# One Trainium2 core, a two-layer hybrid decoder trunk: the first attention unit's scores inside the next product, queries in an even and an odd tile, and a later split of one weight tile

## The chip, the core and the metric

The kernel runs on one core of a Trainium2 chip. A core has five engines with a queue each: TensorE (PE in the profile; its weight loads are PEld), VectorE (DVE), ScalarE (ACT), GpSimd (POOL) and SyncE (SP). Each works through its own queue in order, and semaphores hold an instruction back until what it reads is there. Transfers are issued from the queues of SP, POOL and ACT and run on 16 DMA engines. The metric is the device time of one execution in microseconds (us); lower is better.

## What is computed

A residual stream `x` of 512 tokens by 1024 features goes through two layers in float32. Each layer is a half-weighted SwiGLU, a mixing block and another half-weighted SwiGLU, with an RMSNorm ahead of each and one at the end:

```python
for l in range(2):
    x = x + 0.5 * swiglu(rms_norm(x, ffn1_norm[l]), ffn1_wg[l], ffn1_wu[l], ffn1_wd[l])
    z = rms_norm(x, mix_norm[l]) @ w_in[l]          # 1024 -> q 512 | k 128 | v 128 | conv B, C, h 512 each
    attn = sliding_window_attention(q, k, v, sink)   # 8 query heads of 64, 2 key heads, window 128, blocks of 128 tokens
    conv = B * depthwise_causal_conv3(C * h)
    x = x + concat([attn, conv]) @ w_out[l]
    x = x + 0.5 * swiglu(rms_norm(x, ffn2_norm[l]), ffn2_wg[l], ffn2_wu[l], ffn2_wd[l])   # 1024 -> 2816 -> 1024
return rms_norm(x, final_norm)
```

Attention is computed block by block: a block of 128 queries sees its own 128 keys and the 128 before it, with a linear bias, a learned sink in the softmax's denominator, and probabilities times values.

## The kernel before

**Numbers in two parts.** Every factor of a large product is split into `hi` (a ScalarE cast, line 221, or an activation) and `lo` (what is left, a VectorE subtraction, line 222), and a product is made of three matrix products: hi by hi, hi by lo, lo by hi. So each weight tile of 128x1024 costs ScalarE a cast (`wh<-raw`) and VectorE a subtraction (`wl<-raw,wh`) before TensorE can use it. Weights are loaded into a ring of eight buffers (`raw`, `stock`), which the attention's probability tiles `p` share; `need_split(g)` splits all tiles up to the g-th of a fixed list, and loads four further ahead. `behind(...)` lets instructions be placed only after given others; otherwise a scheduler sets the order on ScalarE and VectorE, and in most places on TensorE.

**The mixing block (`mix`).** `halves` computes keys, values and the first query product in one go. Then come the three other query products (`group(norm.h)`, `j` from 1 to 3, 24 matrix products of 512 columns each; lines 313, 314 and 316), and six pairs of products for the convolution. From each query product, ScalarE copies one half of the partitions and VectorE takes the remainder into the other half, first for the even head (`qe`), then for the odd one (`qo`; lines 1691 and 1692). Attention is cut into eight units, one for each block of queries (four) and key head (two); a unit holds four query heads. `attend(step)` issues the stages of the units that are due in a step: `scores` (eight or so small products into the tiles `sc`, lines 1549 and 1550; then VectorE adds the bias and takes the row maximum, line 1553, and writes `p`; ScalarE takes exponentials, line 1570; VectorE divides, line 1578), then either `turn` (TensorE transposes `pt`, for units 0, 4 and 7) or `apart`, `send` and `join` (two ScalarE copies `pr<-p`, line 1588, a transposing DMA, two ScalarE copies back, line 1609, and the split into `ph` and `pl`, lines 1613 and 1615), and `values` (products `o`, lines 1642 and 1643). The tiles `sc` have two PSUM buffers. The scores of the first unit are issued after query product `j` = 1 and need the heads of `j` = 0 and 1; those of the second unit after `j` = 2.

**From the mixing block into the second SwiGLU.** The output product (`share`) adds into `x` as its parts end. When the last part of a half of the tokens has been added, `Norm.stage` computes the norm of that half: ScalarE's sums of squares, `v` (line 653), ScalarE's reciprocal root `r` (line 654), a Newton step on VectorE (lines 657 and 535 to 537), and the scaled rows `xn` (line 665; two tiles of 128 tokens for each half `o` of the features). TensorE transposes `xn` (`xt`, line 689). `plain_halves` then multiplies by four weight tiles (`held`; products `up`, line 1102), the first half of the tokens first. Between its tiles it pulls the transposes of the second half of the tokens: `o` = 0 after the second tile, `o` = 1 after the third. `hold` splits the third and the fourth of these weight tiles. This transition exists once in each layer, at norms 2 and 5.

**The end (`Finale.down`).** The last two token tiles are closed in an order that is written out by hand for ScalarE and VectorE. The last one is closed in two column pieces; its reciprocal root `r_end` (line 1419) needs `done` (line 1484), which takes in the first piece's sum of squares.

Of the kernel before, what the change touches and what calls it, by code (L numbers as in the profile page):

```python
# [9 lines left out]
F32R = mybir.dt.float32r  # L10
# [6 lines left out]
P = 128  # L17
D = 1024
S = 512
# [56 lines left out]
def trunk_kernel(  # L76
# [254 lines left out]
    def hold(norm, n):  # L331

        first = state["group"]
        if norm.added:
            for ahead, one in ((2, norm.added), (3, norm.first)):
                with behind(one):
                    need_split(first + ahead)
                if norm.later is not None:
                    norm.added = state["sub"]
                    norm.go_on()  # L340
        return [take_split(SPLIT_AHEAD - j)[1:] for j in range(n)]
# [244 lines left out]
    class Norm:  # L586


        def __init__(self, i, gain, mixing, tags):
            self.i, self.row, self.mixing, self.tags = i, gain, mixing, list(tags)  # L590
            self.ss = small(f"ss_{i}", 2 * NT)
            self.seen = [0, 0]
            self.later = self.added = None
            if mixing:
                self.h = None
                return
            self.full = None
# [47 lines left out]
        def stage(self, half):  # L645

            i = self.i
            if half == 0:
                self.rooms()
                self.waiting = []  # L650
            v, r, y = (small(f"{n}_{i}_{half}", 2) for n in "vry")
            at = 2 * half
            nc.vector.tensor_add(v, self.ss[:, at : at + 2], self.ss[:, NT + at : NT + at + 2])
            self.guess = nc.scalar.activation(
                r, v, AF.Abs_reciprocal_sqrt, scale=1.0 / D, bias=eps
            )
            nc.vector.tensor_scalar(v, v, 1.0 / D, EPS, op0=ALU.mult, op1=ALU.add)
            newton(y, r, v)
            self.first = None
            for o in range(2):  # L660
                xns = []
                self.first = self.first or (self.scaled if o else None)
                for t in (at, at + 1):
                    xns.append(g2(f"xn_{i}_{t}_{o}"))
                    self.scaled = nc.vector.scalar_tensor_tensor(
                        xns[-1],
                        xt(t, o),
                        y[:, t - at : t - at + 1],
                        self.gain[o],
                        op0=ALU.mult,  # L670
                        op1=ALU.mult,
                    )
                self.waiting.append((half, o, xns))

        def pull(self):

# [689 lines left out]
    class Finale:  # L1366
# [65 lines left out]
        def down(self, rhs):  # L1432
            for half in range(2):
                gb = g2(f"gain_{half}")
                nc.sync.dma_start(
                    gb, final_norm[half * S : (half + 1) * S].partition_broadcast(P)
                )
                self.gain.append(gb)
            done = small("done", NT)
            self.widen(0, len(rhs) // 2)  # L1440
            for t in range(NT):
                rest = done[:, t : t + 1]
                acc = self.products(rhs, 0, t, 0, S)
                self.close(acc, 0, t, 0, rest)
                nc.vector.tensor_scalar(rest, rest, 1.0 / D, EPS, op0=ALU.mult, op1=ALU.add)
                if t == 0:
                    self.widen(1, len(rhs) // 2)
            def factor(t, ssq):
                return self.root(t, ssq, done[:, t : t + 1])

            def scale(t, by, h):
                y = self.y[t][h]
                if h:
                    nc.vector.scalar_tensor_tensor(
                        y, y, by, self.gain[h], op0=ALU.mult, op1=ALU.mult
                    )
                else:
                    nc.scalar.activation(y, y, AF.Copy, scale=by)
                cols = slice(h * S, (h + 1) * S)
                queue = nc.scalar if h == 0 and t == NT - 1 else nc.sync  # L1460
                queue.dma_start(out[0, t * P : (t + 1) * P, cols], y)

            def piece(t, c0, wide):
                ssq = small(f"ssq_end{t}_{c0}", 1)
                self.close(self.products(rhs, 1, t, c0, wide), 1, t, c0, ssq)
                return ssq

            for t in range(NT - 2):
                by = factor(t, piece(t, 0, S))
                for h in (1, 0):  # L1470
                    scale(t, by, h)


            a, b = NT - 2, NT - 1
            with tc.manual_schedule(engines={act, dve}):
                ssq = piece(a, 0, S)
                early = self.guess(a, ssq, done[:, a : a + 1])
                first = piece(b, 0, H)
                by = self.mend(a, ssq, done[:, a : a + 1], early)
                scale(a, by, 0)  # L1480
                second = piece(b, H, H)
                scale(a, by, 1)
                rest = done[:, b : b + 1]
                nc.vector.scalar_tensor_tensor(
                    rest, first, 1.0 / D, rest, op0=ALU.mult, op1=ALU.add
                )
                by = self.mend(b, second, rest, self.guess(b, second, rest))
                for h in (1, 0):
                    scale(b, by, h)


    def mix(l, norm, after):
# [36 lines left out]
        class Unit:  # L1529
# [8 lines left out]
            def scores(self):  # L1538
# [5 lines left out]
                for i in range(2):  # L1544
                    sc = psum("sc", [P, 2, 2 * P], f"sc_{self.name}_{i}")
                    for j in range(2):
                        h = 2 * i + j
                        qs = q[4 * g + h][:, n * P : (n + 1) * P]
                        nc.tensor.matmul(sc[:, j, lo:], qs, kh[g][:, keys], start=True, stop=False)
                        nc.tensor.matmul(sc[:, j, lo:], qs, kl[g][:, keys], start=False, stop=True)  # L1550
                    for j in range(2):
                        h = 2 * i + j
# [120 lines left out]
        def attend(step, what=(VALUES_AT, TURN_AT, SEND_AT, SCORES_AT)):  # L1673
# [6 lines left out]
                        done = getattr(unit, stages.get(at, "join"))() or done  # L1680
            return done

        for j in range(NH // 2):
            acc = group(norm.h) if j else qacc
            if j == 3:
                vv = take_values()
            if j % 2 == 0:
                room = both(f"q_{l}_{j}", shape=(P, 2, 2, S))
            qe, qo = room[j % 2][:, 0, :], room[j % 2][:, 1, :]
            for z, a, b in ((qe, slice(0, HD), slice(HD, P)), (qo, slice(HD, P), slice(0, HD))):  # L1690
                nc.scalar.activation(z[a, :], acc[a, :], AF.Copy, scale=1.0 / 8.0)
                nc.vector.scalar_tensor_tensor(
                    z[b, :], acc[a, :], 1.0 / 8.0, f32(z[a, :]), op0=ALU.mult, op1=ALU.subtract
                )
            q[2 * j], q[2 * j + 1] = qe, qo
            attend(2 + j)


        step = 6
# [88 lines left out]
```

## Time and profile before

| what | value |
|---|---|
| median of 3 runs | 1639.44 us (1638.18 to 1639.53) |
| the profiled execution's own time | 1638.11 us |
| its span in the trace | 1636.3 us |
| granted TensorE clock, mean | 0.999 of full speed |
| TensorE busy | 1625.2 us, 7544 products |
| VectorE busy | 1303.7 us |
| ScalarE busy | 1144.2 us |
| DMA moved | 310.74 MB, mean 190 GB/s |

A row of the timeline has the start and the duration in microseconds, the engine, the line, the operation, the tiles written and read, the count, and in brackets how long the engine had been idle before it and what ended that. Matrix products are pipelined, so a product's own duration is longer than the distance to the next one's start; distances are taken between starts.

### The profile page before, as it was taken

The numbers are of one execution on the slowest core, as the hardware profiler recorded it, in microseconds if no ns is written. First come the engines' busy times: TensorE is split into PE (matmuls) and PEld (weight loads), VectorE is DVE, ScalarE is ACT, GpSimd is POOL, SyncE is SP. The second block draws the span as 40 slices with busy tenths as digits, with TensorE's granted clock in tenths as the row PEclk, the third lists the DMA queues.
The fourth block names the chain that finished last, engine by engine and source line by source line (L and its number), as shares of the span: only waits on it lengthen the run. The fifth ranks groups of instructions, "written<-read, shape, count | busy, mean of one in ns | idle before, by whom it ended". The sixth has DMA issues, their size and how long they took to land.

```text
span 1636.3 us, 21061 instructions
## 1 busy us (share of the span) xinstructions
PE 1625.2 (99%) x7544; PEld 1353.3 (83%) x7544; DVE 1303.7 (80%) x1718; ACT 1144.2 (70%) x1597; POOL 192.1 (12%) x172
## 2 busy tenths in 40 slices
PE   9999999999999999999999999999999999999998
PEld 7888888888888888888888888888888888888886
DVE  7987779877899867789688677897678987778895
ACT  7457777558867677786476777865597775777864
POOL 0011111100121111112001111110002101111111
PEclk9999999999999999999999999999999999999999
DMA  9379999934685788999737899997147857899991
GB/s 258 89 194 222 225 213 257 220 87 87 176 201 129 206 206 215 213 237 251 217 80 203 211 216 226 226 248 198 40 107 195 209 132 188 216 213 232 222 276 55
DMA packets 295292, 310.74 MB, mean 190 GB/s; under 512 B 116980, under 2 KB 179476, under 8 KB 295188
## 3 DMA queue, kind: packets, MB, share of 16 engines
q1 hardware_dynamic: 252660, 230.09, 49.0%
q0 software_dynamic: 41824, 78.65, 28.1%
q8 instruction: 59, 0.97, 0.2%
q10 hardware_dynamic: 704, 0.66, 0.1%
q14 instruction: 45, 0.37, 0.1%
HBM read 263.74 MB, written 2.10 MB: 162 GB/s over the span
## 4 chain that ended last, share of the span: by engine, by line
PE 88%; ACT 5%; DVE 4%; issue 1%; DMA 1%; SPq 0%; ACTq 0%; DVEq 0%
PE x L945 25%; PE y L945 13%; PE x_s L945 10%; PE w L945 6%; PE y_s L945 5%; PE down L377 3%; PE up L1102 3%; PE w_s L945 3%; PE acc L313 2%; PE acc L314 2%; PE acc L316 2%; PE acc L354 2%; DVE wl L222 1%; PE acc L843 1%; ACT p L1570 1%
## 5 line engine op out<-in xcount | busy, mean ns | idle before, releaser
L222 DVE TENSOR_TENSOR wl<-raw,wh 128x1024 fp32r<-128x1024 f32 (+1 forms) x493 | 599.4, 1220 | 214.1 <-ACT wh L221 212.2
L221 ACT CAST wh<-raw 128x1024 fp32r<-128x1024 f32 (+1 forms) x493 | 512.8, 1044 | 300.1 <-PE y L945 41.8
L945 PE MATMUL x<-wh,ft 128*128 128x512 f32 x608 | 187.1, 389 | 0.0
L945 PE MATMUL y<-wh,ft 128*128 128x512 f32 x608 | 187.1, 389 | 0.0
L945 PE MATMUL x<-wh,fb 128*128 128x512 f32 x608 | 187.1, 389 | 0.0
L945 PEld LDWEIGHTS x<-wh,fb 128*128 128x128 f32 x608 | 114.1, 188 | 23.6
L945 PEld LDWEIGHTS x<-wh,ft 128*128 128x128 f32 x608 | 114.1, 188 | 23.6
L945 PEld LDWEIGHTS y<-wh,ft 128*128 128x128 f32 x608 | 114.1, 188 | 23.6
L945 PE MATMUL x<-wl,fb 128*128 128x512 f32 x304 | 118.3, 389 | 0.0
L945 PE MATMUL x<-wl,ft 128*128 128x512 f32 x304 | 118.3, 389 | 0.0
L945 PE MATMUL y<-wl,ft 128*128 128x512 f32 x304 | 118.3, 389 | 0.0
L216 POOL DMA_DIRECT2D raw<-in_ffn_wu_dram x39 | 47.0, 1215 | 544.1 <-DMA raw<-in_ffn_wu_dram 355.6
L1271 ACT COPY raw_a<-pt 128x1024 uint16<-128x1024 uint16 x76 | 103.2, 1358 | 9.6 <-DMA pt<-pl 9.6
L313 PE MATMUL acc<-hh,wh 128*128 128x512 f32 x240 | 94.2, 392 | 0.0
L314 PE MATMUL acc<-hl,wh 128*128 128x512 f32 x240 | 93.7, 391 | 0.0
L945 PE MATMUL w<-wh,fb 128*128 128x512 f32 x304 | 93.6, 389 | 0.0
L316 PE MATMUL acc<-hh,wl 128*128 128x512 f32 x240 | 93.5, 389 | 0.0
L945 PE MATMUL x_s<-wh,ft_s 128*128 128x512 f32 x256 | 78.8, 389 | 0.0
L945 PE MATMUL y_s<-wh,ft_s 128*128 128x512 f32 x256 | 78.8, 389 | 0.0
L249 DVE TENSOR_TENSOR raw<-raw,raw 128x1024 f32<-128x1024 f32 x58 | 70.3, 1217 | 6.9 <-DMA raw<-in_ffn_wd_dram 6.8
L216 POOL DMA_DIRECT2D raw<-in_ffn_wg_dram x39 | 46.8, 1205 | 234.3 <-DMA raw<-in_ffn_wu_dram 61.8
L945 PE MATMUL x_s<-wh,fb_s 128*128 128x512 f32 x240 | 73.9, 389 | 0.0
(364 smaller groups left out, 3426.2 us busy)
## 6 DMA issues: line engine op xcount, KB each, us to landing
raw<-in_ffn_wu_dram SPq DMA_DIRECT2D x120, 512.0 KB, 5.2
raw<-in_ffn_wd_dram SPq DMA_DIRECT2D x104, 512.0 KB, 6.4
raw<-in_ffn_wg_dram SPq DMA_DIRECT2D x80, 512.0 KB, 5.4
raw<-in_ffn_wu_dram POOLq DMA_DIRECT2D x39, 512.0 KB, 8.3
raw<-in_ffn_wg_dram POOLq DMA_DIRECT2D x39, 512.0 KB, 6.0
raw<-in_w_in_dram SPq DMA_DIRECT2D x36, 512.0 KB, 4.3
raw<-in_ffn_wd_dram POOLq DMA_DIRECT2D x32, 512.0 KB, 8.3
raw<-raw POOLq DMA_DIRECT2D x20, 512.0 KB, 8.2
```

Source lines behind the costliest of these rows:

```text
L216: nc.gpsimd.dma_start(out=r, in_=rows_of(*more), accum_op=ALU.add)
L221: cast = nc.scalar.copy(hi, raw)
L222: state["sub"] = eng.tensor_sub(lo, raw, f32(hi))
L249: nc.vector.tensor_add(a11, a11, s1)
L313: nc.tensor.matmul(acc, hi[:, k, :], rhs[k][0], start=k == first, stop=False)
L314: nc.tensor.matmul(acc, hi[:, k, :], rhs[k][1], start=False, stop=False)
L316: state["product"] = nc.tensor.matmul(acc, lo[:, k, :], rhs[k][0], start=False, stop=k == last)
L354: nc.tensor.matmul(accs[j][:, t * H : (t + 1) * H], w[:, k, :], x_, start=t + k + i == 0, stop=k == KC - 1 and i == 2, skip_group_check=True,)
L377: nc.tensor.matmul(acc, a[:, k, tok], w[:, k, :], start=i + k + n == 0 and fresh[t], stop=i == last and k == 1 and n == 2, skip_group_chec ...
L945: nc.tensor.matmul(accs[u], x_[:, 2 * h + k, tok], w[:, k, :], start=start and h + k + i == 0, stop=h + k == 2 and i == 2, skip_group_chec ...
L1102: nc.tensor.matmul(accs[t], x_[:, tok], w[:, k, :], start=j + k + i == 0, stop=j == 3 and k == 1 and i == 2,)
L1271: nc.scalar.copy(room.rearrange("p c (n z) -> p c z n", z=2)[:, :, z, :], turned[0][:, NT * z + 2 * c : NT * z + 2 * c + 2, :],)
```

## The change

Four edits are made. (1) The first unit's scores (`attend(3)`) are no longer issued after query product `j` = 1, but through the argument `between` inside product `j` = 2, ahead of its seventh weight row (`k == KC - 2`), and the first product of every score is placed behind the product issued last. (2) The queries lie in one tile for even and one for odd heads, each for all four products, instead of one tile for `j` = 0, 1 and one for `j` = 2, 3. (3) At norms 2 and 5 the third weight tile is split behind the first two scaled rows instead of behind the last addition into `x`, and the other two scaled rows follow that split. (4) In `Finale.down` the update of `done` stands ahead of the close of the last piece.

```diff
@@ hold
         if norm.added:
-            for ahead, one in ((2, norm.added), (3, norm.first)):
-                with behind(one):
+            with behind(norm.first if norm.more else norm.added):
+                need_split(first + 2)
+            fourth = norm.first
+            if norm.more:
+                norm.more(state["sub"])
+                norm.more, fourth = None, norm.scaled
+            for ahead in (2, 3):
+                with behind(fourth):
                     need_split(first + ahead)
                 if norm.later is not None:
                     norm.added = state["sub"]
                     norm.go_on()
@@ Norm.stage
-            self.first = None
-            for o in range(2):
+
+            def scale_rows(o):
                 xns = []
-                self.first = self.first or (self.scaled if o else None)
                 for t in (at, at + 1):
                     xns.append(g2(f"xn_{i}_{t}_{o}"))
                     self.scaled = nc.vector.scalar_tensor_tensor(
...
                 self.waiting.append((half, o, xns))
+
+            def more(one):
+                with behind(one):
+                    scale_rows(1)
+
+            scale_rows(0)
+            self.first = self.scaled
+            if half and self.later is not None and not self.mixing:
+                self.more = more
+            else:
+                scale_rows(1)
@@ Finale.down
                 first = piece(b, 0, H)
                 by = self.mend(a, ssq, done[:, a : a + 1], early)
                 scale(a, by, 0)
-                second = piece(b, H, H)
-                scale(a, by, 1)
                 rest = done[:, b : b + 1]
                 nc.vector.scalar_tensor_tensor(
                     rest, first, 1.0 / D, rest, op0=ALU.mult, op1=ALU.add
                 )
+                second = piece(b, H, H)
+                scale(a, by, 1)
@@ Unit.scores
-                        nc.tensor.matmul(sc[:, j, lo:], qs, kh[g][:, keys], start=True, stop=False)
+                        with behind(state["product"]):
+                            nc.tensor.matmul(
+                                sc[:, j, lo:], qs, kh[g][:, keys], start=True, stop=False
+                            )
@@ mix
+        def amid(k, hi, lo):
+            if k == KC - 2:
+                attend(3)
+
+        evens, odds = (
+            xpool.tile([P, NH // 2, S], F32R, tag="xf", bufs=8, name=f"q{n}_{l}") for n in "eo"
+        )
+
         for j in range(NH // 2):
-            acc = group(norm.h) if j else qacc
+            acc = group(norm.h, amid if j == 2 else None) if j else qacc
             if j == 3:
                 vv = take_values()
-            if j % 2 == 0:
-                room = both(f"q_{l}_{j}", shape=(P, 2, 2, S))
-            qe, qo = room[j % 2][:, 0, :], room[j % 2][:, 1, :]
+            qe, qo = evens[:, j, :], odds[:, j, :]
...
-            attend(2 + j)
+            if j != 1:
+                attend(2 + j)
```

What the built programs have in TensorE's queue of the first layer, from the end of query product `j` = 1 on, is first shown as it was; `sc_0_0_0` and `sc_0_0_1` are the first unit's scores of heads 0, 1 and 2, 3, `acc_3277` is product `j` = 2.

```order
L1549 MATMUL sc_0_0_0_3241<-k_3196,q_0_3205 128x128
L1550 MATMUL sc_0_0_0_3241<-k_3196,q_0_3205 128x128
...
L313 MATMUL acc_3277<-hh_0_2838,wh_3155 128x512
L314 MATMUL acc_3277<-hl_0_2839,wh_3155 128x512
L316 MATMUL acc_3277<-hh_0_2838,wl_3156 128x512
...
L1549 MATMUL sc_0_0_1_3248<-k_3196,q_0_3205 128x128
L1550 MATMUL sc_0_0_1_3248<-k_3196,q_0_3205 128x128
```

The same queue of the changed program, where the product is called `acc_3246`, from its sixth weight row on:

```order
L316 MATMUL acc_3246<-hh_1_2840,wl_3156 128x512
L1566 MATMUL sc_0_0_0_3267<-k_3196,qe_3205 128x128
L1569 MATMUL sc_0_0_0_3267<-k_3196,qe_3205 128x128
L1566 MATMUL sc_0_0_0_3267<-k_3196,qo_3206 128x128
L1569 MATMUL sc_0_0_0_3267<-k_3196,qo_3206 128x128
L1566 MATMUL sc_0_0_1_3274<-k_3196,qe_3205 128x128
L1569 MATMUL sc_0_0_1_3274<-k_3196,qe_3205 128x128
L1566 MATMUL sc_0_0_1_3274<-k_3196,qo_3206 128x128
L1569 MATMUL sc_0_0_1_3274<-k_3196,qo_3206 128x128
L313 MATMUL acc_3246<-hh_1_2840,wh_3155 128x512
```

Before, two heads' scores stood straight after product `j` = 1, the third head's after three weight rows of product `j` = 2, and the fourth head's in its fifth row; now all eight products stand together after its sixth row, and two rows follow.

VectorE's queue of the first layer after the second unit's first maxima, before; `nm_1_0` is the second unit's negated maximum, on which ScalarE's exponentials of that unit wait, `q_2` are the queries of product `j` = 2, and `p_0_0` is divided here.

```order
L1553 ISA p_1_0_3308,mx_1_0_3307<-sc_1_0_1_3316,bias,sink 128x256
L1553 ISA mx_1_0_3307 128x1
L1575 RECIPROCAL sums_0_0_3259<-sums_0_0_3259 128x4
L1692 SCALAR_TENSOR_TENSOR q_2_3302<-acc_3277,q_2_3302 64x512
L1578 TENSOR_SCALAR p_0_0_3240<-p_0_0_3240,sums_0_0_3259 128x128 x4
L1692 SCALAR_TENSOR_TENSOR q_2_3302<-acc_3277,q_2_3302 64x512
L1564 TENSOR_SCALAR nm_1_0_3323<-mx_1_0_3307 128x4
```

The same place of the changed program:

```order
L1572 ISA p_1_0_3308,mx_1_0_3307<-sc_1_0_1_3316,bias,sink 128x256
L1572 ISA mx_1_0_3307 128x1
L1583 TENSOR_SCALAR nm_1_0_3323<-mx_1_0_3307 128x4
L1585 TENSOR_TENSOR es_1_0_3325<-sink,nm_1_0_3323 128x4
L1593 TENSOR_TENSOR sums_0_0_3285<-sums_0_0_3285,es_0_0_3283 128x4
L1594 RECIPROCAL sums_0_0_3285<-sums_0_0_3285 128x4
L1597 TENSOR_SCALAR p_0_0_3266<-p_0_0_3266,sums_0_0_3285 128x128 x4
L1717 SCALAR_TENSOR_TENSOR qe_3205<-acc_3246,qe_3205 64x512
L1717 SCALAR_TENSOR_TENSOR qo_3206<-acc_3246,qo_3206 64x512
```

The second unit's maximum now comes ahead of the first unit's division and of the queries of product `j` = 2. On ScalarE, correspondingly, the second unit's exponentials move ahead of the odd copy of product `j` = 2, and the second unit's pair `pr<-p` ahead of the odd copy of product `j` = 3. ScalarE's odd copy of every query product still waits for VectorE's even part of that product, although the two now lie in different tiles.

VectorE's queue at norm 5 (second layer), before; `wl_11434` belongs to the third weight tile and `wl_11441` to the fourth, `xn_2` and `xn_3` are the rows of the second half of the tokens.

```order
L653 TENSOR_TENSOR v_1_11407<-ss_7227 128x2
L222 TENSOR_TENSOR wl_11434<-raw_11182,wh_11433 128x1024
L657 TENSOR_SCALAR v_1_11407<-v_1_11407 128x2
...
L665 SCALAR_TENSOR_TENSOR xn_2_0_11416<-x_90,y_1_11409,gain_0_11054 128x512
L665 SCALAR_TENSOR_TENSOR xn_3_0_11418<-x_90,y_1_11409,gain_0_11054 128x512
L665 SCALAR_TENSOR_TENSOR xn_2_1_11420<-x_92,y_1_11409,gain_1_11055 128x512
L665 SCALAR_TENSOR_TENSOR xn_3_1_11422<-x_92,y_1_11409,gain_1_11055 128x512
L222 TENSOR_TENSOR wl_11441<-raw_11203,wh_11440 128x1024
```

The same place of the changed program, where the third tile's part is `wl_11430`:

```order
L659 TENSOR_TENSOR v_1_11407<-ss_7227 128x2
L663 TENSOR_SCALAR v_1_11407<-v_1_11407 128x2
...
L670 SCALAR_TENSOR_TENSOR xn_2_0_11416<-x_90,y_1_11409,gain_0_11054 128x512
L670 SCALAR_TENSOR_TENSOR xn_3_0_11418<-x_90,y_1_11409,gain_0_11054 128x512
L222 TENSOR_TENSOR wl_11430<-raw_11182,wh_11429 128x1024
L670 SCALAR_TENSOR_TENSOR xn_2_1_11433<-x_92,y_1_11409,gain_1_11055 128x512
L670 SCALAR_TENSOR_TENSOR xn_3_1_11435<-x_92,y_1_11409,gain_1_11055 128x512
L222 TENSOR_TENSOR wl_11441<-raw_11203,wh_11440 128x1024
```

The third tile's subtraction moves from ahead of the Newton step to between the two pairs of rows.

2 lines of the change are left out of this document (1 added, 1 removed).

## The prediction

> **What bounds the kernel now.** I read the page first, then TensorE's waits, the chain of waits, and the timeline at the three places that the change touches.
>
> ```profile
> PE 88%; ACT 5%; DVE 4%; issue 1%; DMA 1%; SPq 0%; ACTq 0%; DVEq 0%
> PE sc L1549 <- DVE q L1692: 1.0, 2, 0.5
> PE xt L689 <- DVE xn L665: 0.8, 2, 0.4
> ```
>
> TensorE is the bound: it holds 88% of the chain that ended last. So an edit can only bring what TensorE loses to waits, and the list of those is short: the scores wait for queries twice, the transposes for scaled rows twice, once in each layer. The chain of waits through the second layer shows where other engines hold the end instead.
>
> ```profile
> 1171.53 0.70 DVE q L1692
> 1172.28 0.33 PE sc L1549
> ...
> 1311.57 0.64 PE xt L689 x4
> ...
> 1312.86 2.74 PE up L1102 x12
> ...
> 1316.48 13.62 PE up L1102 x60
> ```
>
> The path comes to TensorE from VectorE at the first unit's scores and from VectorE's `xn` (the row above) at the transposes. Between the two lies the rest of the mixing block, in which ScalarE, at its densest, has no spare time; this is a window of the first layer:
>
> ```profile
> 400.00:408.00 8.00, 8.00 (x40) 6.77 (x40) 6.62 (x20) 8.00 (x17) 1.30 (x1) 1.00 0.38 94
> ```
>
> The fourth busy time is ScalarE's, 8.00 of 8.00 us. A microsecond won by TensorE at the scores lasts only if ScalarE's and VectorE's work there comes earlier too.
>
> **Scores inside the next product.** These are TensorE's rows around the first unit's scores, and around a later unit of the same shape (`0_1`) that waits for nothing.
>
> ```profile
> 362.71 0.22 PE L1549 MATMUL sc<-k,q 128*128 128x128 f32 x1
> 363.55 0.33 PE L1549 MATMUL sc<-k,q 128*128 128x128 f32 x1 [0.51 <-DVE q L1692]
> ...
> 370.10 0.28 PE L1549 MATMUL sc<-k,q 128*128 128x256 f32 x1
> ...
> 409.88 0.22 PE L1549 MATMUL sc<-k,q 128*128 128x128 f32 x1
> ...
> 411.01 0.40 PE L314 MATMUL acc<-hl,wh 128*128 128x512 f32 x1
> ```
>
> From the first score to the second unit's first score pass 370.10 - 362.71 = 7.39 us, with eight score products and 24 products of 512 columns in them. Undisturbed, a product of 512 columns takes 2.74 / 12 = 0.228 us (the chain's `up` x12), so the eight scores take 411.01 - 0.23 - 409.88 = 0.90, and all together 0.90 + 24 x 0.228 = 6.37. So 1.02 us are lost to waits. Are the queries there in time after the change?
>
> ```profile
> 365.84 0.59 ACT L1691 ACTIVATE q<-acc 64x512 fp32r<-64x512 f32 x1 [1.39 <-DVE q L1692]
> 366.50 0.69 DVE L1692 SCALAR_TENSOR_TENSOR q<-acc,q 64x512 fp32r<-64x512 f32 x1
> ```
>
> The fourth head's queries were finished at 366.50 + 0.69 = 367.19. TensorE now gets to the scores after 18 products, at 362.71 + 18 x 0.228 = 366.81, and to the fourth head six score products later, at about 367.5. It should not wait: the whole 1.02 us per layer goes. The second unit's scores newly wait for the first `sc` buffer; its two maxima of 128 columns start near 367.4 and take less than two of 256 (0.48 each, below), so it is free by 368.4, and TensorE, with two weight rows left, wants it at 366.81 + 0.90 + 6 x 0.228 = 369.08. I cost that at nothing, as I do the other units' new place behind a product, since their rows stand in TensorE's queue as before.
>
> Whether it lasts hangs on ScalarE. It loses time to VectorE now:
>
> ```profile
> 370.77 0.48 DVE L1553 CUSTOM_DVE_ANT_0 p<-sc,bias,sink 128x256 f32<-128x256 f32 x1 [2.02 <-PE sc L1550]
> 373.39 0.60 ACT L1691 ACTIVATE q<-acc 64x512 fp32r<-64x512 f32 x1 [1.49 <-DVE q L1692]
> 375.21 0.51 ACT L1570 ACTIVATE p<-p,nm 128x256 f32<-128x256 f32 x1 [1.22 <-DVE nm L1564]
> 381.06 1.99 ACT L1588 COPY pr<-p 128x1024 uint16<-128x1024 uint16 x2 [0.58 <-DVE p L1578]
> 388.19 0.51 ACT L1570 ACTIVATE p<-p,nm 128x256 f32<-128x256 f32 x1 [0.79 <-DVE nm L1564]
> L222 DVE TENSOR_TENSOR wl<-raw,wh 128x1024 fp32r<-128x1024 f32 (+1 forms) x493 | 599.4, 1220 | 214.1 <-ACT wh L221 212.2
> L221 ACT CAST wh<-raw 128x1024 fp32r<-128x1024 f32 (+1 forms) x493 | 512.8, 1044 | 300.1 <-PE y L945 41.8
> ```
>
> In the new order the second unit's maximum `nm` follows its four maxima at once. They start 0.67 after its first score (370.77 - 370.10), so at 369.08 + 0.67 = 369.75, and end at 369.75 + 4 x 0.48 = 371.67; its exponentials can start at about 371.9 instead of 375.21. ScalarE's queue from there up to the odd copy of product 3: four exponentials (4 x 0.51), two query copies (2 x 0.60), two casts (2 x 1.04), the pair `pr` (1.99), the copy `vv` (about 0.60) and that odd copy (0.60), 8.5 us, to 380.4. Behind it VectorE has that query part and one `pl` (0.69 each), the third unit's last maximum (0.48), two subtractions (2 x 1.22) and the fourth unit's maxima (4 x 0.48): 6.2 us, so the fourth unit's exponentials come at about 386.9 with its small steps, against 388.19: 1.3 us earlier. From there ScalarE runs on without an idle row, so its chain is 1.3 us earlier at the `o` products:
>
> ```profile
> 422.62 0.39 PE L1642 MATMUL o<-ph,vv 128*128 128x512 f32 x1
> 422.99 0.69 DVE L1615 TENSOR_TENSOR pl<-pr,ph 128x512 fp32r<-128x512 f32 x1 [0.15 <-ACT ph L1613]
> 423.73 0.50 PE L1643 MATMUL o<-pl,vv 128*128 128x512 f32 x1
> 424.07 0.60 PE L1625 MATMUL pt<-ident,p 128*128 128x128 f32 x4
> ```
>
> Four products take 424.07 - 422.62 = 1.45 where 4 x 0.228 = 0.91 would do; 0.54 is lost to a late `pl`. TensorE would like to be 1.02 + 0.54 = 1.56 earlier at 424.07, ScalarE's chain allows 1.3. Bounds per layer: 0 if that chain does not move (then `pl` still ends at 423.68), 1.56 if it moves by more. I take **1.3**, twice: 2.6.
>
> The probability tile's new place in the ring moves SP's loads, but no transfer stands in this: the DMA line from 345 to 425, in slices of 2 us, is zero from 363 to 383.
>
> ```profile
> DMA  0000004480000000000939968878600988006988
> ```
>
> **Two tiles of queries.** They change no count or size. Whether they free a wait is the row at 365.84: ScalarE's odd copy, on partitions 64 to 127, waited 1.39 us for VectorE's even part, which reads partitions 0 to 63 of the same product. The built program keeps that wait, so I count nothing. The Trainium skill (PSUM — Partial Sum Buffer, section PSUM bank collisions raise a hardware error) says that two engines must not touch the same bank in the same quadrant of 32 partitions at once, reads included, but that different quadrants of a bank run clean. By that rule the wait would not be needed, and no run here shows it gone; it is a rival below.
>
> **The third weight tile.** Norm 5, VectorE and ScalarE, with TensorE's products before and after the transposes, and the first half's root for its latency:
>
> ```profile
> 1295.80 0.29 ACT L654 ACTIVATE r<-v,eps 128x2 f32<-128x2 f32 x1 [0.23 <-DVE v L653]
> 1296.78 2.74 DVE L665 SCALAR_TENSOR_TENSOR xn<-x,y,gain 128x512 f32<-128x512 f32 x4
> ...
> 1309.01 0.30 ACT L654 ACTIVATE r<-v,eps 128x2 f32<-128x2 f32 x1 [0.32 <-DVE v L653]
> 1310.67 2.74 DVE L665 SCALAR_TENSOR_TENSOR xn<-x,y,gain 128x512 f32<-128x512 f32 x4
> 1310.81 0.39 PE L1102 MATMUL up<-wl,fb 128*128 128x512 f32 x1
> 1312.62 0.71 PE L1102 MATMUL up<-wh,fb 128*128 128x512 f32 x2
> 1313.17 0.39 PE L1102 MATMUL up<-wl,fb 128*128 128x512 f32 x1
> ```
>
> With no subtraction between, the rows start 1296.78 - 1295.80 = 0.98 after the root, at 1309.99 instead of 1310.67, 0.68 earlier. TensorE, free at 1310.81 + 0.23 = 1311.04, finds the first row tile ready, waits a little for the second as now, and starts the third tile's products 0.68 earlier, at 1311.94. The tile's subtraction now starts after two row tiles (1309.99 + 1.37 = 1311.36) and ends at 1312.58; its first use would be at 1313.17 - 0.68 = 1312.49, so about 0.14 is given back. Net **0.54** per layer, 1.08. If the root came no earlier, the subtraction would end at 1313.26 and cost 0.14 instead. The second pair of rows ends at 1312.58 + 1.37 = 1313.95 and is wanted after the third tile's twelve products, at 1312.08 + 2.74 = 1314.8; the fourth tile's subtraction ends at 1315.17 and is wanted behind eight transposes more, 0.5 before the 1316.48 of now or later: both covered. The raw buffer is freed about 2 us later; no wait of TensorE names a transfer after the start, and the next tile is needed only after the 13.62 us of `up`.
>
> **The end.** The root waits for `done`, which stands behind a long row product:
>
> ```profile
> 1627.97 0.19 ACT L1413 ACTIVATION_READ_ACCUMULATOR ysq<-x 128x1 f32 x1
> 1628.19 0.29 ACT L1419 ACTIVATE r_end<-ssq_end,done 128x1 f32<-128x1 f32 x1
> ...
> 1630.32 0.19 ACT L1413 ACTIVATION_READ_ACCUMULATOR ysq<-x 128x1 f32 x1
> 1630.73 0.29 ACT L1419 ACTIVATE r_end<-ssq_end,done 128x1 f32<-128x1 f32 x1 [0.22 <-DVE done L1484]
> ```
>
> Without that wait it follows the sum by 0.22, as at 1628.19, so at 1630.54: **0.19** us, straight on the path to the last store.
>
> **The sum.** 2 x 1.3 + 2 x 0.54 + 0.19 = 3.87 us. The profiled execution took 1638.11 (span 1636.3 and 1.8 around it), which gives 1634.2; it lies 1.33 under the median of 1639.44, and against that the forecast is 1635.5 us. A measurement of this kernel can tell about 0.2%, 3.3 us, from no change, so the forecast stands close to that line.
>
> **Rivals.** ScalarE's chain stays where it is: 8.00 of 8.00 speaks for it, the 1.49, 1.22 and 0.58 of idle before it against. TensorE then waits at `o`, and 1.08 + 0.19 = 1.3 remains: 1638.1 us.
>
> The third tile becomes the wait: the root is not earlier, and each layer loses 0.14. The first half's 0.98 speaks against. 2.6 - 0.28 + 0.19 = 2.5: 1636.9 us.
>
> The wait between the halves of a query product goes: ScalarE's odd copies come up to 1.39 us earlier, its chain moves past 1.56 and TensorE takes all of it. 2 x 1.56 + 1.08 + 0.19 = 4.4: 1635.0 us. The built queue speaks against.
>
> Slower: ScalarE and VectorE lock each other between the second and the fourth unit. ScalarE's odd copy of product 3 now stands behind the pair `pr`, which waits for VectorE's division; VectorE stands behind that copy with the third unit's last maximum. If the four idle rows (1.49 + 1.22 + 0.58 + 0.79 = 4.08) all come back on top of the queue worked out above, the fourth unit's exponentials start at 386.9 + 4.08 = 391.0, 2.8 us later than before, and TensorE pays that at `o` in each layer: 5.6 - 1.27 = 4.3 slower, 1643.8 us. From 0.6 us late it costs more than the rest brings. For it speaks that five hand-overs now follow each other; against it that the maxima come 3 us earlier.
>
> **How the numbers follow.** Forecast 0.52 (0.42 beyond 3.3 us, 0.10 short of it), ScalarE's chain 0.16, third tile 0.13, freed wait 0.03, lock 0.10 (0.08 beyond 3.3 us, 0.02 less), unseen gains of more than 3.3 us 0.04, others within 0.02. Faster 0.42 + 0.03 + 0.04 = 0.49, same 0.10 + 0.16 + 0.13 + 0.02 + 0.02 = 0.43, slower 0.08. The range goes from the largest bounds (1.56 twice, 0.68 twice, 0.19: 4.7, and 0.6 for the difference between runs) at 1634.2 to the ScalarE rival with 0.4 for the runs at 1638.5; the lock lies outside.
>
> **What would show it.** Right: the eight scores follow each other in under 1 us with no wait named for `q`; the fourth unit's exponentials start more than 1 us sooner after the first product's end; the four `o` products take nearer 1.2 us than 1.45; rows `xn` start 0.98 after `r`, with a wait of 0.1 to 0.2 for `wl` in TensorE's list. Wrong: a wait for `pl` at `o` of over 1 us, a wait for `wl` above 0.5, or waits for `raw` that were not there.

## The result, and the profile after

The changed kernel takes 1636.22 us, the kernel before 1639.99 us (medians of 17 runs each). The ratio is 0.9978, with a 95% interval of 0.9970 to 0.9985: 3.6 us saved, 2.5 to 4.9 by the interval. The forecast was 1635.5 us with a sum of 3.87 us. The two profiled executions took 1638.11 and 1635.43 us, 2.68 apart; each lies below its kernel's median, the one of before by 1.88, the one of after by 0.79, so single executions are no measure of a change of this size. I therefore follow the change inside the traces, place by place.

The chain by engine, and TensorE's list of waits after its start, on the page and in the waits view of the changed kernel:

```profile
PE 93%; ACT 5%; DVE 1%; DMA 1%; issue 1%; SPq 0%; ACTq 0%; DVEq 0%
PE x_s L961 <- DVE x L1005: 0.2, 1, 0.2
PE y_m L961 <- ACT wh L221: 0.2, 1, 0.2
```

TensorE holds 93% of the chain instead of 88%, and VectorE 1% instead of 4%. The waits for `q` (1.0 us, twice) and for `xn` (0.8, twice) are gone; two small ones stand in the list that were not there. The second, at `y_m`, will matter. These are TensorE's rows at the first unit's scores in layer 0 (the first, the seventh and the last of the eight, the product behind them, and the second unit's first score), and VectorE's row that the seventh and the eighth need:

```profile
366.92 0.22 PE L1566 MATMUL sc<-k,qe 128*128 128x128 f32 x1
367.54 0.27 PE L1566 MATMUL sc<-k,qo 128*128 128x128 f32 x1
367.65 0.28 PE L1569 MATMUL sc<-k,qo 128*128 128x128 f32 x1
367.76 0.45 PE L313 MATMUL acc<-hh,wh 128*128 128x512 f32 x1
369.21 0.28 PE L1566 MATMUL sc<-k,qe 128*128 128x256 f32 x1
366.61 0.69 DVE L1717 SCALAR_TENSOR_TENSOR qo<-acc,qo 64x512 fp32r<-64x512 f32 x1 [0.66 <-ACT qo L1716]
```

Eight scores take 367.76 - 366.92 = 0.84 us and no wait is named. The fourth head's queries are ready at 366.61 + 0.69 = 367.30, 0.24 us before the product of 367.54 that wants them. ScalarE's rows behind, in the order of its queue:

```profile
371.84 0.51 ACT L1589 ACTIVATE p<-p,nm 128x256 f32<-128x256 f32 x1 [0.55 <-DVE nm L1583]
382.91 1.05 ACT L221 CAST wh<-raw 128x1024 fp32r<-128x1024 f32 x1 [1.94 <-PE acc L314]
387.16 0.51 ACT L1589 ACTIVATE p<-p,nm 128x256 f32<-128x256 f32 x1 [0.64 <-DVE nm L1583]
```

The second unit's exponentials start at 371.84 (forecast: about 371.9, before: 375.21). Then comes something that was not there: 1.94 us of waiting for TensorE to free a weight buffer. The `o` products and the transposes behind them, with the VectorE row they wait for:

```profile
421.74 0.39 PE L1661 MATMUL o<-ph,vv 128*128 128x512 f32 x1
421.93 0.69 DVE L1634 TENSOR_TENSOR pl<-pr,ph 128x512 fp32r<-128x512 f32 x1 [0.16 <-ACT ph L1632]
422.20 0.39 PE L1661 MATMUL o<-ph,vv 128*128 128x512 f32 x1
422.68 0.50 PE L1662 MATMUL o<-pl,vv 128*128 128x512 f32 x1
423.02 0.60 PE L1644 MATMUL pt<-ident,p 128*128 128x128 f32 x4
```

1.28 us for four products, against 1.45 before: one of the two late `pl` is in time now, the second is still waited for by 422.68 - 422.20 - 0.23 = 0.25, and the step behind it is longer by 423.02 - 422.68 - 0.23 = 0.11. At norm 5, ScalarE's root, VectorE's rows and weight remainder, and TensorE:

```profile
1306.98 0.30 ACT L660 ACTIVATE r<-v,eps 128x2 f32<-128x2 f32 x1 [0.33 <-DVE v L659]
1307.96 1.42 DVE L670 SCALAR_TENSOR_TENSOR xn<-x,y,gain 128x512 f32<-128x512 f32 x2
1309.00 1.16 PE L705 MATMUL xt<-ident,xn 128*128 128x128 f32 x8
1309.30 1.22 DVE L222 TENSOR_TENSOR wl<-raw,wh 128x1024 fp32r<-128x1024 f32 x1
1309.91 0.71 PE L1118 MATMUL up<-wh,fb 128*128 128x512 f32 x2
1310.57 0.50 PE L1118 MATMUL up<-wl,fb 128*128 128x512 f32 x1
1310.91 0.61 PE L1118 MATMUL up<-wh,fb 128*128 128x512 f32 x2
```

The rows start 1307.96 - 1306.98 = 0.98 after the root, as forecast. The weight remainder ends at 1309.30 + 1.22 = 1310.52 and holds up the first `wl` product: it starts 0.66 after the first of the two `wh` products, where the kernel before has 0.55 (1312.62 to 1313.17). Last, the end of the kernel:

```profile
1627.83 0.18 ACT L1429 ACTIVATION_READ_ACCUMULATOR ysq<-x 128x1 f32 x1
1628.05 0.29 ACT L1435 ACTIVATE r_end<-ssq_end,done 128x1 f32<-128x1 f32 x1
```

The root follows the sum by 0.22 and waits for nothing.

**Where the time came from.** For the table I take the start of the same TensorE product in the trace of a kernel and in that of before, and write how much the distance changed over each stretch of a layer, layer 0 and layer 1 (minus: won). `Scores` ends behind the second unit's scores, `o` at the transposes `pt` that follow the last `o` products, `out` at the end of the second chain of `y_m` in the mixing block's output product, `norm` behind the transposes of norm 2 or 5. All kernels of the experiments below stand in it, each with its one trace. One execution of e9 took 3336.2 us, twice the others, and is left out of its ratio below.

| kernel | scores | `o` | `out` | norm |
|---|---|---|---|---|
| changed | -1.01, -1.04 | -0.17, -0.16 | +0.07, +0.26 | -0.44, -0.45 |
| e1 scores alone | -1.01, -1.04 | -0.16, -0.17 | +0.27, +0.20 | -0.05, +0.07 |
| e2 third tile alone | 0.00, -0.04 | -0.01, -0.01 | -0.05, +0.02 | -0.48, -0.42 |
| e3 one query tile | -1.01, -1.04 | -0.18, -0.15 | +0.05, +0.29 | -0.48, -0.43 |
| e4 one k later | -1.04, -1.06 | +0.05, +0.05 | +0.34, +0.18 | -0.48, -0.43 |
| e5 one k earlier | -0.46, -0.50 | -0.55, -0.54 | +0.22, -0.01 | -0.46, -0.45 |
| e6 `ph` first | -1.01, -1.04 | -0.42, -0.40 | +0.52, +0.51 | -0.46, -0.42 |
| e7 `wl` last | -1.02, -1.04 | -0.16, -0.16 | +0.18, +0.24 | -0.68, -0.67 |
| e8 e6 and e7 | -1.01, -1.04 | -0.41, -0.43 | +0.60, +0.66 | -0.70, -0.65 |
| e9 later table | -1.01, -1.03 | -0.16, -0.17 | +0.52, +0.26 | -0.09, +0.01 |
| e10 e8 and e9 | -1.01, -1.04 | -0.40, -0.40 | +0.50, +0.70 | -0.28, -0.28 |
| e11 `y_m` emptied first | -1.01, -1.04 | -0.17, -0.16 | -0.18, -0.20 | -0.19, -0.38 |
| e12 e8 and e11 | -1.00, -1.04 | -0.40, -0.40 | -0.18, -0.21 | -0.51, -0.14 |

For the changed kernel the row sums to 2.94; 0.19 at the end makes 3.13. Its profile shows less because it starts 0.13 later and loses 0.32 between the layers, at one wait of 0.35 at 1116.8 that the other traces don't have: 3.13 - 0.13 - 0.32 = 2.68, the difference of the two executions. The same edits with one query tile (e3), without that wait, were profiled at 1634.98, 3.13 below before.

### The profile page after: what moved, and what is told of

Same layout as the page of the kernel before. It is cut to its first block, busy times and chain, and to the rows that moved or that the text cites. A ratio compares the mean times of both kernels' runs of the same rounds, so it can differ in the third digit from the quotient of the medians.

```text
span 1633.7 us, 21063 instructions
## 1 busy us (share of the span) xinstructions
PE 1624.8 (99%) x7544; PEld 1353.7 (83%) x7544; DVE 1304.0 (80%) x1718; ACT 1142.0 (70%) x1597; POOL 192.1 (12%) x172
## 4 chain that ended last, share of the span: by engine, by line
PE 93%; ACT 5%; DVE 1%; DMA 1%; issue 1%; SPq 0%; ACTq 0%; DVEq 0%
PE x L961 25%; PE y L961 13%; PE x_s L961 10%; PE w L961 6%; PE y_s L961 5%; PE up L1118 4%; PE down L383 3%; PE w_s L961 3%; PE acc L313 3%; PE acc L314 3%; PE acc L316 2%; PE acc L360 2%; PE x_m L961 1%; PE xt L705 1%; PE y_m L961 1%; ACT p L1589 1%
```

## The experiments

### e1 and e2: the two large parts alone

```
e1 (before +)  acc = group(norm.h, amid if j == 2 else None) if j else qacc
               ... if j != 1: attend(2 + j); first score product behind(state["product"])
e2 (before +)  hold(): need_split(first + 2) behind norm.first; norm.more(...) behind it
```

> The kernel before with one edit: the first unit's scores inside the query product j=2, at k=6, behind its last product. Theory W, from the trace after: the 1.02 us of waits for `q` go in each layer, and at the last `o` products 0.13 more, since ScalarE waits 1.94 us for a free `wh` buffer at 382.9 and is tied to TensorE again there. So 2 x 1.15 = 2.3 us less than before in the profile, the eight scores within 0.9 us, four `o` products in 1.28 us instead of 1.45. Theory C, as on record: ScalarE's chain has no idle row from the second unit on and passes 1.3 us to `o`: 2.6 us less, and no wait of ScalarE for a `wh` buffer. If the two tiles of queries are needed for the gain: less than 1 us, with waits for `q` still there.

> The kernel before with one edit: the third weight tile at norms 2 and 5 split behind the first two `xn` rows. As on record: rows 0.68 us earlier after the root, a wait for `wl` of about 0.14, net 0.54 per layer, 1.1 us in all. By the trace after: 0.71 gained at the transposes and 0.23 to 0.25 given back at the first products of the tile, net 0.46 per layer, 0.9 us in all. Rival, the third tile becomes the wait: 0.14 lost per layer, 0.3 us slower. Scores and `o` unchanged from before: 1.02 us of waits for `q`, four `o` products in 1.45 us.

Measured: e1 ratio 0.9984 (0.9975 to 0.9993), median 1637.87 against 1640.16; e2 0.9992 (0.9983 to 1.0001), 1639.32. The times add up to the changed kernel's within their intervals but don't size the terms; the table does. Alone, each part brings at its own place what it brings in the changed kernel and nothing at the other's. ScalarE's wait of 1.93 us for a weight buffer stands in e1 too, so theory C's chain without idle rows is out. What neither theory had: e1 gives back 0.20 to 0.27 at `out`, e2 nothing (more on that at e9).

### e3: one query tile again

```
-  qe, qo = evens[:, j, :], odds[:, j, :]
+  if j % 2 == 0: room = both(f"q_{l}_{j}", shape=(P, 2, 2, S))
+  qe, qo = room[j % 2][:, 0, :], room[j % 2][:, 1, :]
```

> The changed kernel with its two query tiles put back to one tile for each pair of products. On record: the two tiles free no wait, so the same time as the changed kernel, within 0.3 us by the profile (scores within 0.9 us, odd copy of ScalarE still 1.39 us behind the even part). Rival, the two tiles carry part of the gain: 1 us or more slower than the changed kernel, with a new wait at the scores or at an odd copy.

Measured: ratio 0.9978 (0.9968 to 0.9989), the changed kernel's, and its row of the table within 0.04 us. The two tiles cost and bring nothing that the traces or the times can tell; the odd copy waits 1.39 us for the even part in both.

### e4 and e5: the scores one k later, one k earlier

```
e4  if k == KC - 1: attend(3)        e5  if k == KC - 3: attend(3)
```

> The changed kernel with the first unit's scores one k later in the product, 0.68 us later. Theory W (ScalarE is tied to TensorE by the 1.94 us wait for a `wh` buffer at 382.9, so what comes before has 1.9 us to spare): the time of the changed kernel within 0.3 us, that wait near 1.3 us, the four `o` products in 1.28 us as in the changed kernel. Theory C (ScalarE's chain has no slack, and every delay of the maxima reaches `o`): 0.68 us later at `o` in each layer, 1.4 us slower than the changed kernel, four `o` products in 1.9 us.

> The changed kernel with the first unit's scores one k earlier in the product, 0.68 us sooner. In the changed kernel VectorE's odd part of the second query product ends at 367.30 and TensorE comes to it at 367.31 at the earliest, so nothing is spare. Theory Q (the place is set by that part): a wait for `qo` of 0.45 to 0.5 us in each layer, and nothing back at `o`: 0.9 to 1.0 us slower than the changed kernel in the profile. Rival: earlier maxima bring ScalarE's chain forward and the `o` products lose no more than 0.1, so that 0.5 us is paid net, or nothing.

Measured: e4 0.9982 (0.9973 to 0.9990), e5 0.9976 (0.9967 to 0.9985). ScalarE's two waits for a weight buffer in e4:

```profile
369.95 1.05 ACT L221 CAST wh<-raw 128x1024 fp32r<-128x1024 f32 x1 [2.60 <-PE acc L314]
383.68 1.06 ACT L221 CAST wh<-raw 128x1024 fp32r<-128x1024 f32 x1 [0.50 <-PE acc L314]
```

The delay of 0.68 arrives at `o` as 0.22 (from -0.17 to +0.05), not as 0 (W) and not as 0.68 (C): most of it is taken up where ScalarE waits, and a part gets through since a `wh` cast moved ahead of the first exponentials and is waited for at 369.95 instead. W is nearer, and not exact. In e5 the wait at the scores is there, and the one at `o` is gone:

```profile
367.67 0.33 PE L1566 MATMUL sc<-k,qo 128*128 128x128 f32 x1 [0.33 <-DVE qo L1717]
...
423.27 0.39 PE L1662 MATMUL o<-pl,vv 128*128 128x512 f32 x1
423.50 0.60 PE L1644 MATMUL pt<-ident,p 128*128 128x128 f32 x4
```

0.55 are lost at the scores and 0.38 come back at `o`. Theory Q had about the loss, but not the return. It let TensorE come to the odd part at 367.31; the product that reads it stands at 367.54 in the changed kernel. So 0.68 - 0.24 = 0.44 had to be waited for, and the other 0.11 lies in the steps behind, as at `o`. The sum up to `pt` is nearly the same for the three places: 1.01 earlier with k one sooner, 1.18 in the changed kernel, 0.99 with k one later. TensorE waits for another engine in each of them, at the scores in e5 and at `o` in the other two, and the chosen k is the best of the three.

### e6, e7, e8: the two waits that were left

```
e6  join(): self.cast = nc.scalar.copy(hi, turned[:, kb])
    go_on(): with behind(last, todo[3].cast if step == 13 else None): need_split(...)
e7  plain_halves(), third tile, first half: terms.sort(key=lambda z: z[2] == 2)   # wl products last
e8  both
```

> The changed kernel with the cast `ph` of the fourth unit's second half put ahead of the `wh` cast that stood before it in ScalarE's queue (row at 420.33, 1.05 us). If the rest of the wait at the last `o` product is only that queue order: `pl` ends 0.25 us or more sooner, the four `o` products take 1.0 us instead of 1.28 in each layer, 0.5 us less than the changed kernel in the profile. Rival: the `wh` cast or the copies behind it come late instead and TensorE waits for a weight tile within the next two products; then nothing is gained or 0.5 us is lost.

> The changed kernel with the products of the third weight tile at the plain norms ordered so that the four with `wl` come after the eight with `wh`. If what is given back at norms 2 and 5 is the wait for the late `wl`: no step between the transposes and the tile's end, 0.23 us less per layer, 0.45 us in all by the profile, and 0.68 to 0.71 gained per norm against the kernel before. Rival: the loss is not the tile but the start of the products behind the transposes; then the same 0.46 per layer as in the changed kernel.

> The changed kernel with both: `ph` ahead of the weight cast and the `wl` products last. If each term is what the rows say, they add: 0.5 + 0.45, about 1 us less than the changed kernel in the profile, 0.06 %, which the times can hardly tell. Rival: the loads of the output weights, which give back 0.24 us at 1285 in the changed kernel, take part of it: 0.5 us.

Measured: e6 0.9976 (0.9967 to 0.9986), e7 0.9977 (0.9968 to 0.9987), e8 0.9974 (0.9964 to 0.9984); medians 1636.05, 1635.61 and 1635.26 against 1639.55. No difference to the changed kernel can be told by time. By the table e6 does at `o` what was expected, 0.24 more, and in its trace 0.5 instead of 0.07 to 0.26 is given back at `out`:

```profile
479.77 0.70 PE L961 MATMUL y_m<-wh,ft_m 128*128 128x512 f32 x2 [0.40 <-ACT wh L221]
```

In e7 the transposes, the eight `wh` products, the four `wl` products and the next transposes follow without a gap:

```profile
501.95 1.16 PE L705 MATMUL xt<-ident,xn 128*128 128x128 f32 x8
502.86 2.09 PE L1120 MATMUL up<-wh,fb 128*128 128x512 f32 x8
504.79 1.08 PE L1120 MATMUL up<-wl,fb 128*128 128x512 f32 x4
505.70 1.04 PE L705 MATMUL xt<-ident,xn 128*128 128x128 f32 x8
```

The norm brings 0.68 and 0.67 instead of 0.44 and 0.45: the late `wl` costs 0.23 per layer. In e8 each stands in its place, and `out` gives 0.6 back.

### e9 to e12: what takes it back at `out`

Up to the second chain of `y_m`, all kernels with moved scores and the old order of the output stage are 0.65 to 1.15 us per layer ahead of before, whether they had won 1.0 or 1.45 at `pt`. Something else sets that point. These are the rows of ScalarE, VectorE and TensorE in the changed kernel's trace ahead of 1285.33:

```profile
1277.67 1.06 ACT L221 CAST wh<-raw 128x1024 fp32r<-128x1024 f32 x1 [1.54 <-DMA raw<-in_w_out_dram]
1282.22 1.22 DVE L222 TENSOR_TENSOR ft_m<-sums_m,ft_m 128x1024 fp32r<-128x1024 f32 x1 [0.89 <-ACT ft_m L221]
1284.22 2.94 ACT L221 CAST wh<-raw 128x1024 fp32r<-128x1024 f32 x3
1284.50 1.28 DVE L1005 SCALAR_TENSOR_TENSOR x<-y_m,x 128x512 f32<-128x512 f32 x2
1285.33 0.70 PE L961 MATMUL y_m<-wh,ft_m 128*128 128x512 f32 x2 [0.19 <-ACT wh L221]
```

ScalarE waits for a load of the output weights, 1.54 us where before it was 1.28; its casts and VectorE's `ft_m` hang on that. This wait accounts for `out`: in the changed kernel and e1 to e10, what it is longer or shorter than before agrees with the table's `out` within 0.05 us in both layers. And it differs between executions. The queues of the changed kernel, e7, e9 and e11 are the same up to that load in layer 0, and ScalarE waits 1.32, 1.44, 1.77 and 1.75 us there. The rows of before (layer 1), of the changed kernel and of e9 (layer 0):

```profile
1279.71 1.06 ACT L221 CAST wh<-raw 128x1024 fp32r<-128x1024 f32 x1 [1.28 <-DMA raw<-in_w_out_dram]
469.94 1.05 ACT L221 CAST wh<-raw 128x1024 fp32r<-128x1024 f32 x1 [1.32 <-DMA raw<-in_w_out_dram]
470.82 1.06 ACT L221 CAST wh<-raw 128x1024 fp32r<-128x1024 f32 x1 [1.77 <-DMA raw<-in_w_out_dram]
```

Through which step does it reach TensorE? Two candidates end together just ahead of 1285.33: the first of the three casts (1284.22 + 1.05 = 1285.27), which the profile names, and the first addition `x<-y_m` (1284.50 + 0.68 = 1285.18), which empties the accumulator that the product writes.

```
e9   Norm.__call__: the table's activation at the third square of norms 2 and 5, not the first
e10  e8 and e9
e11  Seven.make, t4 in the mixing block: nc.scalar.copy(hi, src); the remainder is held back
     share(), step 2:  with behind(added): ops.rest()
e12  e8 and e11
```

> The changed kernel with the loading of the root's table (1.28 us on ScalarE, between the first two squares of norms 2 and 5) moved behind the third square, so that the `wh` cast which TensorE waits for at the first `y_m` product of the output stage comes 1.5 us sooner. If what the scores and `o` bring is cut there (all kernels with the moved scores reach that product 0.8 to 1.1 us earlier than before, whatever they gained at `o`): that wait, 0.13 and 0.35 us in the changed kernel, goes, 0.35 us less in all by the profile. Rival: the table load now stands ahead of the fourth square, the first half's root comes 0.4 us later and TensorE waits for its rows: no gain or a loss of up to 0.8 us.

> The changed kernel with all three: `ph` ahead of the weight cast, the `wl` products last, the table load later. If the wait at the first `y_m` product was what swallowed the 0.25 us gained at `o`: per layer 1.03 at the scores, 0.40 at `o`, nothing given back at `y_m`, 0.68 at the norm, 4.4 us less than before in all by the profile, 1.4 us less than the changed kernel, and no wait of TensorE above 0.2 us from 360 us on. Rival: another step of the output stage is next at the same place and gives back the same 0.25 to 0.5 us per layer: 3.6 us less than before.

Measured: e9 0.9987 (0.9978 to 0.9996), e10 0.9978 (0.9969 to 0.9987). The cast came sooner and the wait stayed (0.57 us in layer 0, 0.35 in layer 1 where the changed kernel had 0.13 and 0.35); the profile now names the other candidate:

```profile
1286.37 0.70 PE L961 MATMUL y_m<-wh,ft_m 128*128 128x512 f32 x2 [0.18 <-DVE x L1005]
```

In e9 the norm, besides, brings 0.09 and nothing; the transposes start 0.25 late again. My reason for the edit fell, and both rivals came true. The next two kernels move the addition instead.

> The changed kernel with one step of VectorE moved at the output stage: the remainder `ft_m` of the operand t4, for which VectorE waits 0.89 us in its queue, comes behind the two additions `x<-y_m` instead of ahead of them. The run with the later table load left the wait at the first `y_m` product where it was and named VectorE's `x<-y_m` for it. If that addition is the cap (it empties the accumulator that the product writes next), it now ends about 2 us sooner, TensorE's waits there (0.13 and 0.35 us in the changed kernel) go, and nothing else moves: 0.3 us less in all by the profile. Rival: the `wh` cast that the profile named in the changed kernel (it ended 0.06 us before the product) is as late: the wait stays above 0.2 us in layer 1 and ScalarE is named.

> The changed kernel with `ph` ahead of the weight cast, the `wl` products last, and VectorE's additions `x<-y_m` ahead of the remainder `ft_m`. If that addition was what took back the 0.25 us gained at `o`: per layer 1.03 at the scores, 0.40 at `o`, nothing back at `y_m`, 0.68 at the norm; 4.4 us less than before in all by the profile, 1.3 us less than the changed kernel. Rival: the `wh` cast behind the table load is next at the same place, since TensorE now comes there 0.25 us sooner: 0.3 to 0.6 us per layer given back, 3.4 us less than before.

Measured: e11 0.9980 (0.9971 to 0.9989), e12 0.9968 (0.9956 to 0.9981), median 1634.17 against 1639.01. In e11, layer 1:

```profile
1282.59 1.28 DVE L1009 SCALAR_TENSOR_TENSOR x<-y_m,x 128x512 f32<-128x512 f32 x2
1284.41 2.94 ACT L221 CAST wh<-raw 128x1024 fp32r<-128x1024 f32 x3
1285.19 0.62 PE L965 MATMUL y_m<-wh,ft_m 128*128 128x512 f32 x2
```

The addition ends 2 us sooner and TensorE goes through without a gap, while the first of the three casts still ends at about 1284.41 + 1.05 = 1285.46, behind the product's start. So the cast was never what `y_m` waited for; the profile had named the one of two that ended last. ScalarE's wait for the load is no shorter in e11 (1.75 and 1.53 us) and e12 (1.66 and 1.99): it no longer reaches TensorE there. `out` now brings 0.2 per layer instead of costing 0.07 to 0.26. A part of that is lost at the norm (0.19 and 0.38 instead of 0.45). e12 keeps 0.40 at `o`; its table sums to 3.88, which with the 0.19 at the end and 0.28 between the layers is 4.35 of the 4.4 expected. That the sum agrees is luck: `out` brings 0.39 that was not counted, the norms 0.65 instead of 1.36, and the 0.28 is traced to no edit. It is the fastest of all; its median (5 runs) is 2 us below that of the changed kernel, measured beside other runs of before, and the two intervals overlap, so that it beats the changed kernel is what the trace says and the time alone doesn't settle. Its last wait, named in TensorE's list, is at the transposes of norm 5:

```profile
PE xt L705 <- ACT hf L721: 0.2, 1, 0.2
```

## Why the prediction was right or wrong, step by step

**Scores: right, shown.** 1.02 per layer were to go; 1.01 and 1.04 went, alone (e1) and together. The place has 0.24 us to spare and no more (e5).

**What it brings at `o`: right in kind, too large.** 0.28 per layer was counted (1.3 less the 1.02), 0.16 came. The step that failed is "from there ScalarE runs on without an idle row". The row at 382.91 shows 1.94 us of idle time in that stretch: ScalarE came early enough to run into the limit of four `wh` buffers, whose release is TensorE's time. The fourth unit's exponentials come 1.17 sooner after the last product of query product `j` = 1 (387.16 - 362.62 against 388.19 - 362.48), not 1.3. Of the 0.37 still lost at `o` (1.28 less 4 x 0.228), 0.24 was the order of ScalarE's queue just ahead (e6), which the prediction did not look at.

**Two tiles: right.** Nothing moved, and e3 shows it. That the wait of 1.39 us between the two halves of a product is not needed was not tried.

**Third tile: right in kind, the give-back too small.** 0.68 was forecast as won and 0.14 as given back. Won were 0.68 (e7), given back 0.23. The prediction's own two times, 1312.58 and 1312.49, are 0.09 apart; its 0.14 holds 0.05 more, for which it gives no row; as much lies between the end of the remainder and the product in the trace (1310.52 to 1310.57). The wait itself is 0.11; the second 0.11 lies in the step behind the product that waited (last section). No wait of `raw` appeared.

**The end: right.** The root follows its sum by 0.22, the 0.19 is there.

**What was missing.** The sum let everything that is won at `o` reach the end. In the output stage 0.07 and 0.26 of it were lost again, behind a load that ScalarE waits for 0.05 and 0.26 longer. The prediction followed ScalarE up to the `o` products and stopped there. At the next place where another engine's chain meets TensorE, 55 us on, TensorE waited already before (0.09 us, 1287.05 + 0.23 to 1287.37 in layer 1), so whatever comes later there is paid in full. Since that wait for the load differs by up to 0.45 between executions of the same queues, the 0.33 belongs to this trace, and is not shown to belong to the change.

So the errors are 0.23 at `o`, 0.19 at the norms and 0.33 at `out`, 0.75 together, and 3.87 - 0.75 = 3.1 is what the traces show of the change. The times say 3.6 with an interval of 2.5 to 4.9, which holds both; that 3.6 lies nearer to the forecast doesn't make these terms right. Of the rivals, the first (ScalarE's chain stays) has a true core: its exponentials moved 1.17 and not 1.3. The third tile as the wait is there with 0.23 of 0.68. The lock of ScalarE and VectorE did not come: ScalarE had about 2 us to spare where it was feared.

Open remains why that load is waited for longer. In layer 1 of the changed kernel it was issued 2.3 us earlier and the cast behind it came only 2.04 earlier. The next load was issued 3.5 us behind it instead of 3.8, but that is not the reason: in layer 0 of the kernel before it is 3.5 too, with a wait of 1.27 us, and in layer 1 of e5 it is 3.5 with a wait of 1.28. In layer 1 the four kernels with `ph` first wait 1.82 to 1.99 us and all others 1.28 to 1.59, so the edits may have a part in it; in layer 0 the two groups overlap (1.66 to 1.86 and 1.20 to 1.77). With one trace of each kernel, no run separates the edit from the execution.

## What to carry to other kernels

After a wait of the bounding engine is removed, go on to the next place where another engine's chain joins it, and look there for a wait of almost zero: whatever comes later at such a place is paid in full. Here that took 0.33 us in the trace, as much as had been won at `o`. A gain of a few tenths of a microsecond is followed by the starts of the same instruction in two traces, stretch by stretch; at the scores, `o` and the norms these agreed within about 0.05 us between kernels with the same edit, where the medians could not tell 1 us. At `out`, behind a transfer, they did not: there one trace of each kernel is too little. And when two producers end within 0.15 us of the consumer's start, the name in the profile is not evidence: move one and see whether the wait stays.

## What the runs showed of the hardware

In these traces a wait of TensorE cost more than its own length. Behind the late `wl`, the product that waited takes 0.50 instead of 0.39, and the next one starts 0.34 later (1310.57 to 1310.91) instead of 0.23 (1313.17 to 1313.40 in the kernel before). The wait of 0.11 so cost about 0.2, and with the wait gone (e7) both parts were back. The same step of 0.34 stands behind the late `pl` (422.68 to 423.02), and of 0.23 there in e5, where nothing is late (423.27 to 423.50).

The start of the kernel also differs from one execution to the next, though the queues are the same up to there: the product at 345 us stood 0.13 to 0.92 us later than in the trace of before in most kernels, and 2.1 and 2.3 in two, which waited 1.1 and 0.9 us for a `wl` at 265. The largest of these is two thirds of the 3.6 us that the change saves.
